# Output-projection weights: three plain quarters split on chip by every tile instead of stored split

## The chip, the cores and the metric

The kernel runs on one core of one Trainium2 chip. The metric is the device time of one execution in microseconds. The kernel before takes 2673.55 us (median of 3 runs, 2673.15 to 2673.85). The five compute engines of the core are named as in the profile: PE multiplies matrices (PEld is its weight loading), DVE is the vector engine, ACT the scalar engine, POOL the general-purpose engine, and SP issues the DMA transfers. Each engine works through its own list of instructions in order, and waits on semaphores for the others.

## The reference, cut to what matters

The reference is a two-layer encoder trunk on a sequence of 2048 rows and width 1024, all in float32. Layer A is a gated mixer. From its result a shared K and V are projected. Layer B is a chunked band attention with a gate, an output projection and a residual, and a last norm follows.

```
q, z = jnp.split(h @ w_qz, 2, axis=-1)
...
p = jax.nn.softmax(sc, axis=-1).astype(vc.dtype)
return jnp.einsum('bhqk,bkhd->bqhd', p, vc)
...
return (o * jax.nn.silu(z)) @ w_out
```

The change concerns only the last matrix product, with the 1024 x 1024 weight `w_out` of layer B, which the kernel knows as `wb_out`.

## The kernel before

**Tiles and pairs.** Layer B works on four tiles t = 0 to 3 of 512 rows. In each tile it goes through eight pairs p = 0 to 7 of attention heads (heads 2p and 2p+1). For a pair, PE projects Q, K and the gate (`pj`), forms the scores (`s`), transposes the normalised probabilities (`tp`) and multiplies them with V (`pv`). For each 128-row block of a head, DVE adds the bias and takes the row extreme (`pr` and `nm`), ACT applies the exponential, DVE inverts the sum (`sl`), POOL scales the row (`pr`), PE transposes, ACT copies the transposed block out (`pt`) and DVE subtracts the copy from it to get its low part (`pt`). The output projection of tile t-1 (`bo`) is dealt out in small portions among the pairs of tile t. `SHARE` says how many portions go into which pair. The last tile's own output projection (`bo_`, function `last_all`) comes at the end.

**Number format.** A float32 operand is split into a high part, which is a cast to fp32r on ACT, and a low part, which is a subtraction on DVE. Each product is then three matmuls: high by high, high by low, low by high.

**Output projection by seven products.** The weight is cut into four quarters b11, b12, b21, b22, each 512 x 512, and each quarter into halves q = 0, 1 of 128 partitions x 1024 elements (512 KB). A tile's product is Strassen's scheme with seven products in the order 1, 7, 2, 6, 5, 4, 3. Products 1, 2 and 3 use a plain quarter of the weight (b11, b21, b22). Products 4 to 7 use sums of quarters.

**Where the split weights come from.** During the first four pairs of tile t = 1, `o_sums` loads the quarters in four units of 128 x 512 each, lets POOL form the sums, splits all seven operands (cast on ACT, subtraction on DVE, tiles `so`), and stores high and low part in DRAM, in `ows[ph, q]`. From then on `o_right(t)` loads four tiles per product, `wh_bo` and `wl_bo` for q = 0 and 1, each 512 KB, straight into the ring with tag "T". That ring has 8 buffers, and the split projection weights `wh_b` and `wl_b` of the attention pairs live in it too. In the last tile `last_right` places weights in various buffers that are free by then. There product 2 alone already loads its plain quarter raw and splits it.

**The projection weights of a pair.** `weights` loads a 512 KB raw tile (`raw_b`) into the ring with tag "wr", which has 2 buffers (`raw_w`), and `split_in` casts it on ACT (`wh_b`, line 230 before) and subtracts on DVE (`wl_b`, line 231 before).

**What sets the order.** The code is written as generators that are interleaved by counts. A scheduler then orders each engine's list. All loads and stores named here are issued by SP, so a load whose buffer is not yet free holds up what stands behind it in SP's list. `on_beat` and `paced_by_pj` tie an instruction to the order of a PE instruction.

Names in the profile have their tile numbers left out: `wl_bo` is the low weight of any tile's output projection, `wlbo` or `wbo` that of the last tile.

Of the kernel before, what the change touches and what calls it, by code (L numbers as in the profile page):

```python
# [9 lines left out]
F32 = mybir.dt.float32  # L10
# [7 lines left out]
P = 128  # L18
# [15 lines left out]
def trunk_kernel(  # L34
# [19 lines left out]
    nc = tc.nc  # L54
# [10 lines left out]
    }  # L65
    ows = {
        (ph, q): dram.tile([P, 2, 1024], F32, name=f"ows{ph}_{q}")
        for ph in range(1, 8) for q in range(2)
    }
    owf = [dram.tile([P, 1024], F32, name=f"owf{q}") for q in range(2)]  # L70
    khd = [
        [dram.tile([2, P, T], F32, name=f"khd{t}_{p}") for p in range(NPAIR)]
        for t in range(NT - 1)
# [121 lines left out]
    def on_beat(ins):  # L195
        if beat:
            tc.add_manual_dep(
                ins.ins, beat[-1],
                mybir.DependencyInfo(mybir.DependencyClass.NoSync, mybir.DependencyReason.DATA),
                reason="order",  # L200
            )
        return ins
# [21 lines left out]
    def raw_w(t, name):  # L224
        if t:
            return raws[0].tile([P, 1024], F32, tag="wr", name=name, bufs=2)
        return sh.tile([P, 1024], F32, tag="raw", name=name, bufs=4)

    def split_in(raw, wh, wl):
        hi = nc.scalar.copy(wh[:], raw[:])  # L230
        tv(wl[:], raw[:], wh[:].bitcast(F32), op=sub)  # L231
        return hi
# [22 lines left out]
        return w  # L255

    o_early = {}

    def o_right(t):
        def right(ph):  # L260
            if (t, ph) in o_early:
                return o_early.pop((t, ph))
            out = []
            for q in range(2):
                name = f"bo{t}_{ph}_{q}"
                w = [w_tile(f"w{i}_{name}") for i in "hl"]
                for i in range(2):
                    nc.sync.dma_start(w[i][:].bitcast(F32), ows[ph, q][:, i, :])
                out.append(w)
            return out  # L270
        return right
# [68 lines left out]
    def o_sums(u, place, s_place):  # L340

        q, i = divmod(u, 2)
        cs = slice(i * 512, i * 512 + 512)
        w = {}
        for rc in ((0, 0), (0, 1), (1, 1), (1, 0)):
            w[rc] = place(f"wo{u}_{rc[0]}{rc[1]}")
            paced_by_pj(nc.sync.dma_start(w[rc][:], wb_out[rc[0], rc[1], q][:, cs]))
        b11, b12, b21, b22 = (w[k][:] for k in ((0, 0), (0, 1), (1, 0), (1, 1)))

        pend = []  # L350

        def stores():
            while pend:
                on_beat(nc.sync.dma_start(*pend.pop(0)))

        def keep(ph, src):
            stores()
            if ph == 5:
                pend.append((owf[q][:, cs], src))
            hi, lo = (s_place(f"so{u}_{ph}{x_}") for x_ in "hl")  # L360
            on_beat(nc.scalar.copy(hi[:], src))
            tv(lo[:], src, hi[:].bitcast(F32), op=sub)
            for n, y_ in enumerate((hi, lo)):
                pend.append((ows[ph, q][:, n, cs], y_[:].bitcast(F32)))

        def first():
            keep(1, b11)
            on_beat(tg(b11, b12, b11, op=sub))
            on_beat(tg(b12, b22, b12, op=sub))

        def second():
            keep(3, b22)
            on_beat(tg(b22, b22, b11, op=sub))

        def third():
            keep(2, b21)
            on_beat(tg(b21, b21, b22, op=sub))

        return [first, second, third] + [
            lambda ph=ph, o=o: keep(ph, o)  # L380
            for ph, o in ((5, b11), (7, b12), (6, b22), (4, b21))
        ] + [stores]

    with ExitStack() as actx:
        ca = actx.enter_context(tc.tile_pool(name="ca", bufs=1))

# [885 lines left out]
    with ExitStack() as bctx:  # L1272
# [310 lines left out]
        def last_right(ph, q):  # L1583
            name = f"bo_{ph}_{q}"
            if ph == 5:
                v = sb.tile([P, 8, 256], F32R, tag="V", name=f"w{name}", bufs=2)
                w = [v[:, i * 4 : i * 4 + 4, :].rearrange("p a b -> p (a b)") for i in range(2)]
            elif ph == 3:
                if q == 0:
                    lw["pt"] = sb.tile([P, 5376], F32R, tag="PT", name=f"w{name}", bufs=1)  # L1590
                w = [lw["pt"][:, (2 * q + i) * 1024 : (2 * q + i + 1) * 1024] for i in range(2)]
            elif ph == 2:
                w = [
                    sh.tile([P, 1024], F32R, tag="raw", name=f"w{i}{name}", bufs=4)[:]
                    for i in "hl"
                ]
            else:
                w = [w_tile(f"w{i}{name}")[:] for i in "hl"]
            if ph == 2:
                raw = raw_w(NT - 1, f"raw_{name}")  # L1600
                nc.sync.dma_start(raw[:], wb_out[1, 0, q])
                nc.scalar.copy(w[0], raw[:])
                tv(w[1], raw[:], w[0].bitcast(F32), op=sub)
            else:
                for i in range(2):
                    nc.sync.dma_start(w[i].bitcast(F32), ows[ph, q][:, i, :])
            lw[ph, q] = w
# [232 lines left out]
        first = ahead(0, 0)  # L1840
# [105 lines left out]
```

## Time and profile before

| what | value |
|---|---|
| median of 3 runs | 2673.55 us |
| the profiled execution, its own time | 2677.64 us |
| its span on the core | 2675.7 us |
| mean granted PE clock | 0.993 |
| PE busy | 2615.7 us, 98% |
| DVE busy | 1872.6 us, 70% |
| ACT busy | 1288.6 us, 48% |
| POOL busy | 895.9 us, 33% |
| DMA queue q1 | 735.19 MB, 79.9% of 16 engines |

The profile is of one execution. Its own time is 4.09 us above the median of the runs, and 1.9 us above its span. Times in its rows are microseconds from the start of the span. Layer B's tile 1 begins at about 1690 us, and everything that the change touches lies between there and the end. A busy PE is not PE at its peak, since matmuls overlap and their ends are modelled, so lost PE time is read from stretches in which PE is not busy and from the granted clock.

### The profile page before, as it was taken

What the parts mean: (1) busy time and instruction counts of PE and PEld (TensorE: products, weight loads), DVE (VectorE), ACT (ScalarE), POOL (GpSimd) and SP (SyncE); (2) the same over time, 40 slices, a digit from 0 to 9 for tenths busy, and PEclk for the clock granted to TensorE, in tenths of its full rate; (3) what the DMA queues carried; (4) which work ended last, traced back from release to release, by engine and by line L of the source; (5) the groups of instructions that cost most, each with busy time, mean ns of one, the idle gap of its engine ahead of it and who ended that gap; (6) DMA issues with size and microseconds to landing.
All of it is one profiled execution on the core that took longest, in us unless ns stands there. A gap on an engine that the chain in (4) does not pass through costs nothing. (4 is left out here: it accounts for less than half of the span.)

```text
span 2675.7 us, 38056 instructions
## 1 busy us (share of the span) xinstructions
PE 2615.7 (98%) x12960; PEld 2187.7 (82%) x12960; DVE 1872.6 (70%) x2934; ACT 1288.6 (48%) x2293; POOL 895.9 (33%) x874
## 2 busy tenths in 40 slices
PE   8999999999999999999999999999999999999997
PEld 7888888888888888888878778887888888888886
DVE  5655676766777577757776767787767677877676
ACT  5422242443433435433355456666655555655563
POOL 3511335152252413104134344333343233323235
PEclk9999999999999999999999999999999999999999
DMA  7899999989988879858676587789788766875678
GB/s 295 314 323 333 348 363 326 320 309 360 325 311 295 311 243 332 319 193 286 255 260 221 188 266 224 233 288 302 252 275 278 247 210 213 265 233 181 205 227 298
DMA packets 281057, 737.61 MB, mean 276 GB/s; under 512 B 29600, under 2 KB 69536, under 8 KB 280864
## 3 DMA queue, kind: packets, MB, share of 16 engines
q1 hardware_dynamic: 280864, 735.19, 79.9%
q8 instruction: 103, 1.69, 0.2%
q14 instruction: 90, 0.74, 0.1%
HBM read 542.65 MB, written 181.93 MB: 271 GB/s over the span
## 5 line engine op out<-in xcount | busy, mean ns | idle before, releaser
L113 PE MATMUL P<-T,S 128*128 128x512 f32 x1248 | 496.2, 398 | 2.0 <-ACT S L434 2.0
L115 PE MATMUL P<-T,S 128*128 128x512 f32 x1248 | 490.4, 393 | 0.0
L114 PE MATMUL P<-T,S 128*128 128x512 f32 x1248 | 489.1, 392 | 1.1 <-DVE T L437 1.1
L1405 POOL TENSOR_SCALAR pr<-pr,sl 128x640 f32<-128x640 f32 (+4 forms) x256 | 202.7, 792 | 528.9 <-DVE sl L1404 468.7
L113 PE MATMUL pj<-hh_b,wh_b 128*128 128x512 f32 x768 | 318.5, 415 | 0.0
L115 PE MATMUL pj<-hh_b,wl_b 128*128 128x512 f32 x768 | 305.5, 398 | 3.6 <-DVE wl_b L231 3.4
L114 PE MATMUL pj<-hl_b,wh_b 128*128 128x512 f32 x768 | 303.4, 395 | 0.0
L1401 ACT ACTIVATE pr<-pr,nm 128x640 f32<-128x640 f32 (+4 forms) x256 | 195.4, 763 | 176.0 <-DVE nm L1394 174.0
L115 PEld LDWEIGHTS P<-T,S 128*128 128x128 f32 x1248 | 235.4, 189 | 50.3
L113 PEld LDWEIGHTS P<-T,S 128*128 128x128 f32 x1248 | 235.8, 189 | 47.0 <-ACT S L434 2.2
L114 PEld LDWEIGHTS P<-T,S 128*128 128x128 f32 x1248 | 235.8, 189 | 46.9 <-DVE T L437 1.3
L1426 DVE TENSOR_TENSOR pt<-tp,pt 128x640 fp32r<-128x640 f32 (+4 forms) x256 | 188.3, 736 | 46.0 <-ACT pt L1425 43.6
L1394 DVE CUSTOM_DVE_ANT_0 pr<-s,bias 128x640 f32<-128x640 f32 (+4 forms) x256 | 187.9, 734 | 41.9 <-PE s L1386 37.4
L1425 ACT CAST pt<-tp 128x640 fp32r<-128x640 f32 (+4 forms) x256 | 158.8, 620 | 53.0 <-PE tp L1421 50.2
L1421 PE MATMUL tp<-ident,pr 128*128 128x128 f32 x1120 | 167.2, 275 | 11.0 <-DVE pt L1426 8.6
L115 PEld LDWEIGHTS pj<-hh_b,wl_b 128*128 128x128 f32 x768 | 144.8, 189 | 37.6 <-DVE wl_b L231 6.0
L1421 PEld LDWEIGHTS tp<-ident,pr 128*128 128x128 f32 x1120 | 131.0, 141 | 45.3 <-issue 18.2
L1446 PEld LDWEIGHTS pv<-pt,V 128*128 128x128 f32 x896 | 145.1, 191 | 25.1 <-DVE pt L1426 6.2
L1446 PE MATMUL pv<-pt,V 128*128 128x256 f32 (+3 forms) x896 | 157.4, 323 | 5.7 <-DVE pt L1426 3.8
L113 PEld LDWEIGHTS pj<-hh_b,wh_b 128*128 128x128 f32 x768 | 145.8, 190 | 18.8 <-ACT wh_b L230 1.4
L114 PEld LDWEIGHTS pj<-hl_b,wh_b 128*128 128x128 f32 x768 | 145.8, 190 | 17.4
L231 DVE TENSOR_TENSOR wl_b<-raw_b,wh_b 128x1024 fp32r<-128x1024 f32 x96 | 125.2, 1305 | 29.1 <-ACT wh_b L230 27.5
(297 smaller groups left out, 5698.6 us busy)
## 6 DMA issues: line engine op xcount, KB each, us to landing
S<-hsd SPq DMA_DIRECT2D x288, 512.0 KB, 5.5
rw<-in_w_a SPq DMA_DIRECT2D x108, 512.0 KB, 6.4
A<-ytd SPq DMA_DIRECT2D x72, 512.0 KB, 5.8
raw_b<-wk SPq DMA_DIRECT2D x72, 512.0 KB, 4.3
hsd<-S SPq DMA_DIRECT2D x56, 512.0 KB, 4.3
V<-vhd SPq DMA_DIRECT2D x56, 512.0 KB, 5.4
wh_bo<-ows SPq DMA_DIRECT2D x42, 512.0 KB, 5.3
wl_bo<-ows SPq DMA_DIRECT2D x42, 512.0 KB, 5.8
```

The costliest lines, as they stand in the source:

```text
L113: first = mm(ps, lh, rh, start=first, stop=False)
L114: mm(ps, lh, rl, start=False, stop=False)
L115: mm(ps, ll, rh, start=False, stop=last)
L231: tv(wl[:], raw[:], wh[:].bitcast(F32), op=sub)
L1394: nc.vector.tensor_tensor_reduce(out=pr[:, c0:].rearrange("p (a b) -> p a b", a=nseg), in0=ps[:, :nseg, :w], in1=bias[:, c0:].rearrange("p ...
L1401: nc.scalar.activation(pr[:, c0:], pr[:, c0:], AF.Exp, scale=-1.0, bias=nm[:], accum_out=sl[:])
L1405: nc.gpsimd.tensor_scalar(pr[:, c0:], pr[:, c0:], sl[:], 1.0, op0=ALU.mult, op1=ALU.mult)
L1421: ins = tpose(tp[:, b, :], pr[:, b * P : (b + 1) * P], ident[:])
L1425: nc.scalar.copy(oh, tp[:, b0:5, :].rearrange("p a b -> p (a b)"))
L1426: nc.vector.tensor_tensor(pt[:, 2560 + o + b0 * P : 2560 + o + 640], tp[:, b0:5, :].rearrange("p a b -> p (a b)"), oh.bitcast(F32), op=ALU ...
L1446: mm(po[:, q0 * P : q1 * P], vtl[t, p][:, i, hs], rhs, start=(i == blocks[0] and j == 0), stop=(i == 7 and j == 1),)
```

## The change

`ows` keeps only products 4 to 7, the four sums. For products 1, 2 and 3 every tile now loads the plain quarter raw from the weight itself, two loads of 512 KB instead of four, into the 2-buffer "wr" ring, and splits it with `split_in` into the same T buffers as before. `o_sums` no longer splits and stores the three plain quarters, so per unit three casts, three subtractions and six stores of 256 KB go. A seventh store, of the raw sum for product 5 into `owf`, which nothing read, goes as well. The POOL sums now run one after the other in the first places of a unit. In the last tile products 1 and 3 are loaded raw and split as product 2 already was.

Counted over the program: in `o_sums` 12 casts and 12 subtractions of 128 x 512 go, with 28 stores of 256 KB. Added are 22 casts and 22 subtractions of 128 x 1024: 18 of each in tiles 0 to 2 and 4 in the last tile. In tiles 0 to 2, 18 raw loads take the place of 36 loads, and in the last tile 4 take the place of 8, all of 512 KB.

```diff
--- before.py
+++ after.py
@@ -65,9 +65,8 @@
     }
     ows = {
         (ph, q): dram.tile([P, 2, 1024], F32, name=f"ows{ph}_{q}")
-        for ph in range(1, 8) for q in range(2)
+        for ph in range(4, 8) for q in range(2)
     }
-    owf = [dram.tile([P, 1024], F32, name=f"owf{q}") for q in range(2)]
     khd = [
         [dram.tile([2, P, T], F32, name=f"khd{t}_{p}") for p in range(NPAIR)]
         for t in range(NT - 1)
@@ -255,6 +254,7 @@
         return w
 
     o_early = {}
+    o_raw = {1: (0, 0), 2: (1, 0), 3: (1, 1)}
 
     def o_right(t):
         def right(ph):
@@ -264,8 +264,13 @@
             for q in range(2):
                 name = f"bo{t}_{ph}_{q}"
                 w = [w_tile(f"w{i}_{name}") for i in "hl"]
-                for i in range(2):
-                    nc.sync.dma_start(w[i][:].bitcast(F32), ows[ph, q][:, i, :])
+                if ph in o_raw:
+                    raw = raw_w(1, f"raw_{name}")
+                    nc.sync.dma_start(raw[:], wb_out[o_raw[ph]][q])
+                    split_in(raw, *w)
+                else:
+                    for i in range(2):
+                        nc.sync.dma_start(w[i][:].bitcast(F32), ows[ph, q][:, i, :])
                 out.append(w)
             return out
         return right
@@ -355,32 +360,21 @@
 
         def keep(ph, src):
             stores()
-            if ph == 5:
-                pend.append((owf[q][:, cs], src))
             hi, lo = (s_place(f"so{u}_{ph}{x_}") for x_ in "hl")
             on_beat(nc.scalar.copy(hi[:], src))
             tv(lo[:], src, hi[:].bitcast(F32), op=sub)
             for n, y_ in enumerate((hi, lo)):
                 pend.append((ows[ph, q][:, n, cs], y_[:].bitcast(F32)))
 
-        def first():
-            keep(1, b11)
-            on_beat(tg(b11, b12, b11, op=sub))
-            on_beat(tg(b12, b22, b12, op=sub))
-
-        def second():
-            keep(3, b22)
-            on_beat(tg(b22, b22, b11, op=sub))
-
-        def third():
-            keep(2, b21)
-            on_beat(tg(b21, b21, b22, op=sub))
-
-        return [first, second, third] + [
-            lambda ph=ph, o=o: keep(ph, o)
-            for ph, o in ((5, b11), (7, b12), (6, b22), (4, b21))
+        def combine(o, x_, y_):
+            return lambda: on_beat(tg(o, x_, y_, op=sub))
+
+        return [
+            combine(b11, b12, b11), combine(b12, b22, b12), combine(b22, b22, b11),
+            lambda: (keep(5, b11), on_beat(tg(b21, b21, b22, op=sub))),
+        ] + [
+            lambda ph=ph, o=o: keep(ph, o) for ph, o in ((7, b12), (6, b22), (4, b21))
         ] + [stores]
-
     with ExitStack() as actx:
         ca = actx.enter_context(tc.tile_pool(name="ca", bufs=1))
 
@@ -1596,9 +1590,9 @@
                 ]
             else:
                 w = [w_tile(f"w{i}{name}")[:] for i in "hl"]
-            if ph == 2:
+            if ph in o_raw:
                 raw = raw_w(NT - 1, f"raw_{name}")
-                nc.sync.dma_start(raw[:], wb_out[1, 0, q])
+                nc.sync.dma_start(raw[:], wb_out[o_raw[ph]][q])
                 nc.scalar.copy(w[0], raw[:])
                 tv(w[1], raw[:], w[0].bitcast(F32), op=sub)
             else:
```

**SP's list at product 3 of tile 0.** Here `bo0_3_0` is tile 0, product 3, half 0; `oc0` and `or0` are pieces of tile 0's result, `x2d0` its place in DRAM, `x1d0` the residual, and `reld` the attention bias. Before:

```order
L268 DMA wl_bo0_4_0_18741<-ows4_0_108 128x1024
L268 DMA wh_bo0_4_1_18744<-ows4_1_109 128x1024
L268 DMA wl_bo0_4_1_18745<-ows4_1_109 128x1024
L1483 DMA x2d0_1_155<-oc0_110_18710 128x512
L1665 DMA oc0_111_18770<-x1d0_60 128x512
L1665 DMA or0_101_18777<-x1d0_60 128x512
L1665 DMA or0_011_18780<-x1d0_60 128x512
L1363 DMA bias1_15_18807<-reld15_181 128x640
L268 DMA wh_bo0_3_0_18851<-ows3_0_106 128x1024
L1483 DMA x2d0_3_157<-oc0_111_18770 128x512
L268 DMA wl_bo0_3_0_18852<-ows3_0_106 128x1024
```

and now, in SP's list, the raw quarter's two loads:

```order
L273 DMA wl_bo0_6_1_18288<-ows6_1_107 128x1024
L244 DMA raw_b1_7_0_18438<-wk7_0_85 128x1024
L1477 DMA x2d0_0_146<-oc0_000_18254 128x512
L1659 DMA oc0_001_18311<-x1d0_60 128x512
L269 DMA raw_bo0_3_0_18777<-in_wb_out 128x1024
L177 DMA xr_b2_0_18914<-xtd2_140 128x4x256
L1477 DMA x2d0_2_148<-oc0_001_18311 128x512
L269 DMA raw_bo0_3_1_18783<-in_wb_out 128x1024
L1337 DMA V1_7_18523<-vhd0_134 128x1024
```

The loads for product 3 stood behind the store of `oc0_111`, which is late in the tile. They now stand ahead of the loads for products 5 and 4, between the stores of product 2's results. What comes later is the split, in ACT's list (its DVE half stands at a like place), where `pt1_13` and `pr1_14` are the softmax of heads 13 and 14:

```order
L1419 CAST pt1_13_18591<-tp1_13_1_18647 128x640
L1674 ACTIVATE jk0_110_18655,ssq0_1_18638<-oc0_110_18634 128x512
L229 CAST wh_bo0_3_0_18775<-raw_bo0_3_0_18777 128x1024
L1395 ACTIVATE pr1_14_0_18681,sl1_14_0_18683<-pr1_14_0_18681,nm1_14_0_18682 128x640
L333 CAST Sho0_4_1_18724<-A0_11_18191 128x512
L1419 CAST pt1_13_18591<-tp1_13_2_18707 128x640
L229 CAST wh_bo0_3_1_18781<-raw_bo0_3_1_18783 128x1024
```

The casts stand in the middle of that softmax, with the exponential and the copy of transposed blocks behind each of them.

**SP's list ahead of the last tile.** `A_hh` are the last tile's left operands, read from DRAM (`ogd3`), `bo2_3` and `bo2_4` weights of tile 2's last products. Before:

```order
L268 DMA wh_bo2_4_1_25032<-ows4_1_109 128x1024
L268 DMA wl_bo2_4_1_25033<-ows4_1_109 128x1024
L268 DMA wh_bo2_3_0_25112<-ows3_0_106 128x1024
L1483 DMA x2d2_3_165<-oc2_111_25054 128x512
L268 DMA wl_bo2_3_0_25113<-ows3_0_106 128x1024
L268 DMA wh_bo2_3_1_25116<-ows3_1_107 128x1024
L1483 DMA x2d2_1_163<-ou2_7_0_23208 128x512
L268 DMA wl_bo2_3_1_25117<-ows3_1_107 128x1024
L1532 DMA A_hh_25120<-ogd3_153 128x1024 x2
L1532 DMA A_hh_25120<-ogd3_153 128x512 x2
L1487 DMA x2d2_3_165<-ou2_7_1_23569 128x512
```

and now:

```order
L273 DMA wh_bo2_4_1_24980<-ows4_1_103 128x1024
L273 DMA wl_bo2_4_1_24981<-ows4_1_103 128x1024
L1526 DMA A_hh_25072<-ogd3_145 128x1024
L1477 DMA x2d2_3_157<-oc2_111_25002 128x512
L1526 DMA A_hh_25072<-ogd3_145 128x1024
L1526 DMA A_hh_25072<-ogd3_145 128x512
L1477 DMA x2d2_1_155<-ou2_7_0_23152 128x512
L1526 DMA A_hh_25072<-ogd3_145 128x512
L1595 DMA raw_bo_1_0_25198<-in_wb_out 128x1024
```

The four loads for `bo2_3` are gone from this place, since their raw loads stand earlier, and the loads of `A_hh` moved up behind `wl_bo2_4_1`.

**DVE's list at the end of the program.** `row0` to `row3` are the four row blocks of the last tile's result, `bo_4` and `bo_3` its last products, `Qlo` the low parts of left operands, and `rr_f` the norm factor. Before:

```order
L1751 TENSOR_TENSOR ou3_1_1_25463<-bo_5_1_25700,ou3_1_1_25463 128x512
L331 TENSOR_TENSOR Qlo_3_0_25732<-A_hl_25121,Qho_3_0_25731 128x512
L331 TENSOR_TENSOR Qlo_3_1_25760<-A_hl_25121,Qho_3_1_25759 128x512
L1768 TENSOR_TENSOR row1_25559<-bo_4_0_25724,ou3_7_0_25520 128x512
L1768 TENSOR_TENSOR row3_25561<-bo_4_1_25752,ou3_7_1_25573 128x512
L1700 TENSOR_TENSOR rr_f3_1_25744<-ssq3_1_25694 128x1
L127 TENSOR_SCALAR rr_f3_1_25744<-rr_f3_1_25744 128x1
L1718 SCALAR_TENSOR_TENSOR row1_25559<-row1_25559,rr_f3_1_25744,gf_13539 128x512 x2
L1700 TENSOR_TENSOR rr_f3_3_25772<-ssq3_3_25718 128x1
L127 TENSOR_SCALAR rr_f3_3_25772<-rr_f3_3_25772 128x1
L1718 SCALAR_TENSOR_TENSOR row3_25561<-row3_25561,rr_f3_3_25772,gf_13539 128x512 x2
L1768 TENSOR_TENSOR row0_25490<-bo_3_0_25780,ou3_1_0_25423 128x512
```

and now:

```order
L1597 TENSOR_TENSOR wbo_3_0_25568<-raw_bo_3_0_25569,wbo_3_0_25568 128x1024
L1762 TENSOR_TENSOR row1_25515<-bo_4_0_25684,ou3_7_0_25476 128x512
L336 TENSOR_TENSOR Qlo_3_0_25692<-A_hl_25073,Qho_3_0_25691 128x512
L1597 TENSOR_TENSOR wbo_3_0_25568<-raw_bo_3_1_25573,wbo_3_0_25568 128x1024
L1694 TENSOR_TENSOR rr_f3_1_25704<-ssq3_1_25654 128x1
L336 TENSOR_TENSOR Qlo_3_1_25720<-A_hl_25073,Qho_3_1_25719 128x512
L126 TENSOR_SCALAR rr_f3_1_25704<-rr_f3_1_25704 128x1
L1762 TENSOR_TENSOR row3_25517<-bo_4_1_25712,ou3_7_1_25529 128x512
L1712 SCALAR_TENSOR_TENSOR row1_25515<-row1_25515,rr_f3_1_25704,gf_13531 128x512 x2
L1694 TENSOR_TENSOR rr_f3_3_25732<-ssq3_3_25678 128x1
L126 TENSOR_SCALAR rr_f3_3_25732<-rr_f3_3_25732 128x1
L1762 TENSOR_TENSOR row0_25446<-bo_3_0_25740,ou3_1_0_25379 128x512
```

The split of `wbo_3` (two subtractions) entered the list, `row1` moved ahead of `Qlo_3_0`, and `row0` no longer waits behind the scaling of `row3`.

## The prediction

> **What bounds the kernel now.** I read the summary first, then the waits of PE from 1690 us on, then busy time in stretches of 25 us, then single instructions around each loss. The summary's first row says that PE is the bound:
>
> ```profile
> PE 2615.7 (98%) x12960; PEld 2187.7 (82%) x12960; DVE 1872.6 (70%) x2934; ACT 1288.6 (48%) x2293; POOL 895.9 (33%) x874
> ```
>
> The matmuls stay as many as they are. So only what PE loses, and what stands behind its last matmul, can change the time. The losses after 1690 us, by releaser (columns: total, times, longest):
>
> ```profile
> PE tp L1421 <- DVE pt L1426: 6.5, 10, 2.2
> PE bo L114 <- DMA wl_bo<-ows: 4.7, 3, 2.3
> PE pv L1446 <- DVE pt L1426: 3.3, 3, 1.4
> PE pj L115 <- DVE wl_b L231: 2.9, 2, 2.3
> PE pv L1446 <- ACT pt L1425: 1.8, 1, 1.8
> ```
>
> The second row is a wait for exactly the weights that the change touches. The others are the softmax and the weight splits, which compete for ACT and DVE. The stretches (busy time of PE, PEld, DVE, ACT, POOL, each with a count, then granted clock, DMA share, GB/s) place them:
>
> ```profile
> 1675.00:1700.00 25.00, 24.67 (x130) 20.63 (x129) 18.09 (x44) 16.12 (x38) 10.57 (x16) 1.00 0.72 229
> ...
> 1775.00:1800.00 25.00, 23.66 (x128) 19.42 (x127) 21.60 (x40) 17.27 (x31) 11.26 (x14) 1.00 0.88 299
> 1800.00:1825.00 25.00, 24.20 (x136) 20.08 (x135) 19.52 (x37) 16.77 (x32) 8.76 (x11) 1.00 0.92 312
> 1825.00:1850.00 25.00, 22.98 (x132) 19.48 (x131) 19.63 (x38) 17.17 (x33) 7.65 (x13) 1.00 0.96 309
> 1850.00:1875.00 25.00, 22.67 (x117) 18.44 (x116) 18.54 (x32) 15.62 (x27) 9.74 (x11) 0.93 0.86 283
> ...
> 1950.00:1975.00 25.00, 22.87 (x122) 19.14 (x121) 14.93 (x28) 14.26 (x28) 10.25 (x11) 1.00 0.82 257
> ...
> 2000.00:2025.00 25.00, 21.69 (x107) 18.00 (x106) 15.66 (x30) 13.65 (x27) 7.52 (x9) 0.93 0.84 279
> 2025.00:2050.00 25.00, 23.78 (x128) 20.08 (x126) 22.69 (x38) 14.99 (x26) 11.43 (x11) 1.00 0.86 297
> ...
> 2600.00:2625.00 25.00, 22.79 (x124) 19.67 (x123) 21.00 (x41) 13.83 (x31) 15.32 (x16) 0.93 0.98 354
> ```
>
> The sums are made between 1700 and 1875 us. There DVE, ACT and DMA are all fuller than before or after, and PE loses 0.8 to 2.3 us per stretch against 0.33 in the quiet row at 1675. Three stretches also ran at a clock of 0.93, each after a stall of some 2 us. I count 7% of 25 us, 1.75 us, for such a clock.
>
> **Term 1, the sums.** A unit loses three casts and three subtractions of these groups (mean ns before the second bar), and seven stores:
>
> ```profile
> L361 ACT CAST so_1h<-wo 128x512 fp32r<-128x512 f32 x4 | 2.5, 622 | 0.1
> ...
> L362 DVE TENSOR_TENSOR so_1l<-wo,so_1h 128x512 fp32r<-128x512 f32 x4 | 2.8, 692 | 0.1
> ...
> L362 DVE TENSOR_TENSOR so_2l<-wo,so_2h 128x512 fp32r<-128x512 f32 x4 | 2.9, 737 | 0.0
> ...
> L362 DVE TENSOR_TENSOR so_3l<-wo,so_3h 128x512 fp32r<-128x512 f32 x4 | 4.4, 1111 | 0.0
> ```
>
> That is 12 x 0.62 = 7.4 us of ACT and 2.8 + 2.9 + 4.4 = 10.1 us of DVE. None of it is on PE's path by itself. What it costs there is what the four stretches from 1775 to 1875 lose above the quiet row: 1.01 + 0.47 + 1.69 + 2.00 = 5.2 us, with the clock 6.9. The dearest of these stalls reads:
>
> ```profile
> 1853.56 1.19 SPq L354 DMA_DIRECT2D ows<-so_1h  x1
> ...
> 1856.77 0.81 SPq L245 DMA_DIRECT2D raw_b<-wk  x1
> ...
> 1863.93 1.04 ACT L230 CAST wh_b<-raw_b 128x1024 fp32r<-128x1024 f32 x1 [3.02 <-DMA raw_b<-wk]
> 1865.00 0.69 ACT L1425 CAST pt<-tp 128x640 fp32r<-128x640 f32 x1
> ...
> 1865.74 0.50 PE L1446 MATMUL pv<-pt,V 128*128 128x512 f32 x1 [1.76 <-ACT pt L1425]
> ```
>
> A raw weight took 7.1 us among the stores of `so_1` and `so_3`. Its cast held up ACT, the copy `pt` stood behind the cast, and `pv` waited for that. The stores go, so I take most of it: -5.0 us, between 0 (POOL's sums and the other four splits stay in the same pairs) and -6.9.
>
> **Term 2, the late plain weights.** The two big waits of PE for `wl_bo` are both for plain quarters, products 2 and 3 of tile 0:
>
> ```profile
> 1956.47 0.50 PE L114 MATMUL bo<-wl_bo,Sho 128*128 128x512 f32 x1 [2.00 <-DMA wl_bo<-ows]
> ...
> 2009.42 0.50 PE L114 MATMUL bo<-wl_bo,Sho 128*128 128x512 f32 x1 [2.25 <-DMA wl_bo<-ows]
> ```
>
> Their stretches lose 25 - 22.87 = 2.13 and 25 - 21.69 = 3.31 us, with the clock in the second 5.44 + 1.75 = 7.2. They are late because the load cannot start before PE gives a T buffer back, and then takes its time:
>
> ```profile
> SPq L268 <- PE pj L115: 70.2, 25, 6.1
> ...
> DMA to landing us min/median/max: 3.7/5.8/8.8
> ...
> L231 DVE TENSOR_TENSOR wl_b<-raw_b,wh_b x75: 1204/1225/2339, 1690.1 to 2573.0; 128x1024 fp32r<-128x1024 f32 x75
> ...
> L230 ACT CAST wh_b<-raw_b x75: 1030/1049/1065, 1689.0 to 2571.9; 128x1024 fp32r<-128x1024 f32 x75
> ```
>
> Before, buffer to weight is 5.8 us. Afterwards the raw tile can be there already, since it needs a "wr" buffer and not a T buffer, and from buffer to weight are a cast of 1.05 and a subtraction of 1.23 us, 2.3 us. That is 3.5 us less, more than either wait. I take -7.0 us, between 0 and -7.2.
>
> **Term 3, the 22 new splits.** They put 22 x 1.05 = 23.1 us on ACT and 22 x 1.33 (99.5 us over 75 in the group of `wl_b` with its slow ones; 29.2) on DVE, in stretches from 1880 to 2660 us. In stretches like 1675, where DVE is busy for 18 of 25 us, PE is nearly full, so part of them is hidden by waiting room in the softmax. For a price per split I take all that PE waited in this part for `pt` and `wl_b`, 6.5 + 3.3 + 2.9 + 1.8 = 14.5 us, over the 75 splits that are there now: 0.19 us. Times 22: +4.3 us, between 0 and 1 us each (+22, the bound that the first rival needs).
>
> **Term 4, the tail.** The stall around 2611 us starts from the transfers of `A_hh`, issued behind the `bo2_3` loads:
>
> ```profile
> 2598.55 0.95 SPq L1532 DMA_DIRECT2D A_hh<-ogd  x1
> ...
> 2607.15 2.54 POOL L1539 TENSOR_TENSOR A_hl<-A_hh 128x512 f32<-128x512 f32 x2 [5.89 <-DMA A_hh<-ogd]
> ...
> 2611.47 1.75 DVE L1718 SCALAR_TENSOR_TENSOR y<-y,rr_f,gf 128x512 f32<-128x512 f32 x1 [0.56 <-POOL rr_f L128]
> ...
> 2613.14 0.81 DVE L1426 TENSOR_TENSOR pt<-tp,pt 128x640 fp32r<-128x640 f32 x1
> ```
>
> POOL's sum `A_hl` came late, behind it the norm factor of `y`, behind that on DVE `y` itself, and behind `y` the `pt` that PE waited for. With `A_hh` issued about 7 us earlier and `pt` ahead of `y`, I count -2.0 of this stretch's 2.21 + 1.75, because four new splits enter a DVE that is busy for 21 of 25 us here. After the last matmul the chain ends on DVE:
>
> ```profile
> 2664.94 1.42 DVE L1718 SCALAR_TENSOR_TENSOR row<-row,rr_f,gf 128x512 f32<-128x512 f32 x2 [0.66 <-POOL rr_f L128]
> ...
> 2666.27 1.28 DVE L1768 TENSOR_TENSOR row<-bo,ou 128x512 f32<-128x512 f32 x2
> ```
>
> `row0` and `row2` stood behind the scaling of `row3`. Now `row0` goes ahead of it, and one scaling (1.42) with part of a hand-over leaves the path: -1.7 us. Together -3.7, between -5.7 (all of both) and +3 (two of the new splits, 2 x 1.3 us, land on the path at `wbo_3`).
>
> **The rest.** 18 loads of 512 KB fewer up to 2600 us (two for one, 9.4 MB) and 4 fewer in the last tile cost nothing and are worth nothing by themselves, since SP and DMA are hidden except where named. The stretch at 2025, where DVE is busy for 22.69 of 25 us, sees its casts in another order, with `A` loads earlier: 0, between -1 and +2.
>
> **The sum.** -5.0 - 7.0 + 4.3 - 3.7 = -11.4 us. The profiled execution took 2677.64 us, 4.09 above the median of the runs, and its span is 2675.7. The terms are differences, so the profiled one would come to 2666.2 and the median to 2673.55 - 11.4 = 2662.2 us.
>
> **A price for meeting POOL.** One row speaks against term 3, a split beside a long operation of POOL:
>
> ```profile
> 2268.16 3.52 POOL L1758 TENSOR_TENSOR ou<-ou,or 128x512 f32<-128x512 f32 x2
> ...
> 2268.19 2.34 DVE L231 TENSOR_TENSOR wl_b<-raw_b,wh_b 128x1024 fp32r<-128x1024 f32 x1
> ```
>
> The subtraction took 2.34 us against the median of 1.225 quoted above. The mean of 1.33 says that this is rare: 0.10 us on average, already in term 3. If each of the 22 met POOL in this way, they would cost 22 x 1.11 = 24.4 us, in place of 4.3 (fourth rival).
>
> The Trainium skill, page "SBUF — State Buffer", section "SBUF: two separate sides", says that a vector operation with two operands in SBUF and a GpSimd operation that reads SBUF hold a shared pair of ports exclusively, the loser waiting for the whole instruction. This row agrees with that, and the new subtractions are of this kind; the median of the other rows says that most do not meet such an operation.
>
> **Rivals.** First, slower: the wait for a free T buffer moves from SP, where nothing but transfers stands behind it, to ACT. If a new cast finds its buffer or its raw tile late, the exponential and `pt` stand behind it, as at 1863.93 us. There it cost 2.0 us of PE and 1.75 of clock, 3.75 us. The gains are 15.7 us, so from five casts in 22 on it decides. Six would cost 22.5: 2673.55 - 15.7 + 22.5 = 2680.4 us. Against it: today ACT's casts wait little:
>
> ```profile
> ACT wh_b L230 <- PE pj L114: 15.7, 11, 1.8
> ```
>
> Second, no change: term 1 is 0 because POOL's sums set the stalls there, term 2 gives 5 and the tail nothing: -5 + 4.3, 2672.9 us. Third, the shared 2-buffer ring makes the pairs' own raw weights late. SP already waits for it:
>
> ```profile
> SPq L245 <- DVE wl_b L231: 34.5, 11, 9.4
> ```
>
> PE's longest wait for `wl_b` is 2.3 us. Six such waits, 13.8, give 2673.55 - 11.4 + 13.8 = 2676.0 us. Fourth, every new subtraction meets POOL and takes 2.34 in place of 1.23 us, and PE pays that: -15.7 + 22 x 1.11 = +8.7, 2682.3 us. Fifth, all terms at their good ends and the splits hidden: -6.9 - 7.2 - 5.7 = -19.8, 2653.8 us.
>
> **Chances.** Forecast 0.48, first 0.14, second 0.17, third 0.10, fourth 0.04, fifth 0.07. About 0.2%, 5.3 us, can be told from no change. Faster takes the forecast but 0.01 and the fifth, 0.54; same takes that 0.01, the second and most of the third, 0.25; slower the rest, 0.21. The range is 2652 to 2680. It takes in the fifth and reaches up to the first, leaving out the fourth, half of the first and what lies beyond. The forecast's own range is 2656 to 2668.
>
> **What would show it.** Term 1: PE over 24 in the stretches from 1775 to 1875. Term 2: no PE wait for products 2 and 3 of tile 0, and `wl_bo` on DVE near 1.3 us. Term 3: PE's waits for `pt` up by some 4 us. Term 4: `A_hl` started some 5 us or more ahead of its place among the rows around it, and the last scaling nearer to the last matmul. The prediction is wrong if ACT stands idle before casts of `wh_bo` for more than 1 us each, with PE waiting for `pt` behind them.

## The result

The changed kernel takes 2661.46 us (median of 6 runs, 2659.12 to 2664.78) against 2673.68 us for the kernel before (6 runs, 2672.29 to 2678.3). The ratio is 0.9949, with a 95% interval of 0.9938 to 0.9960: 12.2 us, or 0.5%, faster. Two later comparisons on other chips gave 0.9938 (0.9925 to 0.9951) and 0.9953 (0.9940 to 0.9967), with medians 16.9 and 13.6 us apart. The profiled execution took 2663.55 us, its span 2661.8 us, 13.9 us below the span before.

### The profile after, by stages

The milestones in both traces are the first transposition of head 0 in tile 1 (the sums begin around it), tile 0's first output product, the first transposition of tile 2, the one of head 13 in tile 3 (the tail begins), and the last matmul. The view of stretches, cut near these points, shows per stretch the busy time of PE, PEld, DVE, ACT and POOL with counts, then clock, DMA share and GB/s. Before:

```profile
1750.00:1910.00 160.00, 153.24 (x836) 128.00 (x835) 126.49 (x230) 104.78 (x189) 56.95 (x71) 0.99 0.90 292
1910.00:2059.00 149.00, 142.33 (x752) 121.04 (x751) 102.87 (x187) 84.11 (x154) 56.36 (x63) 0.99 0.81 267
2059.00:2583.00 524.00, 517.05 (x2835) 443.56 (x2833) 380.20 (x693) 304.79 (x552) 154.91 (x211) 1.00 0.68 219
2583.00:2664.00 81.00, 78.55 (x393) 65.53 (x391) 58.22 (x104) 38.88 (x80) 42.39 (x40) 0.98 0.88 322
```

After:

```profile
1748.00:1898.00 150.00, 149.20 (x838) 127.98 (x837) 119.28 (x221) 99.59 (x179) 58.04 (x70) 1.00 0.82 261
1898.00:2040.00 142.00, 140.54 (x756) 120.05 (x754) 109.13 (x189) 87.94 (x159) 57.42 (x63) 1.00 0.79 260
2040.00:2566.00 526.00, 517.85 (x2828) 443.73 (x2827) 387.88 (x702) 312.43 (x561) 156.42 (x210) 1.00 0.66 208
2566.00:2652.00 86.00, 79.63 (x395) 65.24 (x393) 70.94 (x116) 46.55 (x89) 47.06 (x41) 0.98 0.78 273
```

The same matmuls, to a few records that the cuts move, take 10 us less during the sums and 7 us less in tile 0's product, and 5 us more in the tail. DVE shows where the work went: 7.2 us less during the sums, 6.3 more in tile 0's product, 7.7 more in tiles 2 and 3, and 12.7 more in the tail, where the six new subtractions alone take 10.9 us.

The exact times between the milestones, from every trace of this case (us; the last matmul is taken at its start; the runs are told below):

| kernel | sums | tile 0's product | tiles 2, 3 | tail, PE | after the last matmul |
|---|---|---|---|---|---|
| before | 159.7 | 149.1 | 524.3 | 80.7 | 11.9 |
| changed, three profiles | 149.2, 149.9, 149.9 | 141.9, 141.9, 142.1 | 527.1, 521.9, 522.9 | 85.0, 85.1, 84.9 | 10.5, 10.4, 10.4 |
| e1, sums as before | 159.6 | 141.6 | 522.9 | 85.1 | 10.8 |
| e2, last tile only | 158.0 | 149.4 | 525.0 | 84.9 | 9.5 |
| e3, sums only | 149.7 | 146.6 | 524.4 | 81.7 | 11.8 |
| e4, stores only | 152.8 | 147.7 | 524.8 | 81.9 | 11.8 |
| e5, tail stored | 149.5 | 142.8 | 523.7 | 80.8 | 11.8 |
| e6, only tile 2 stored | 149.7 | 142.1 | 521.4 | 86.7 | 9.5 |
| e7, subtraction twice | 148.9 | 143.8 | 527.8 | 85.3 | 10.5 |
| e9 and its repetition | 149.5, 149.0 | 142.3, 141.4 | 522.3, 522.6 | 81.4, 81.3 | 11.8, 11.8 |
| e10, one tile split | 149.6 | 144.2 | 525.1 | 80.8 | 11.9 |

What stands before the first milestone is the same work in all of them, and still the first milestone lies between 1746.1 and 1751.0 us. That scatter is not the change's. Of the 13.9 us in span, 1.9 are of this kind.

### Where PE was held up before and is not now

The same stretches of 25 us as in the prediction, of the changed kernel:

```profile
1775.00:1800.00 25.00, 25.00 (x145) 21.98 (x144) 18.95 (x38) 16.47 (x31) 12.71 (x16) 1.00 0.82 266
1800.00:1825.00 25.00, 25.00 (x142) 21.34 (x141) 20.71 (x38) 16.54 (x30) 12.65 (x15) 1.00 0.81 259
1825.00:1850.00 25.00, 24.46 (x141) 20.93 (x140) 19.49 (x37) 16.23 (x29) 9.14 (x12) 1.00 0.91 302
1850.00:1875.00 25.00, 25.00 (x144) 21.63 (x143) 21.45 (x41) 19.43 (x37) 9.27 (x12) 1.00 0.74 232
...
1950.00:1975.00 25.00, 25.00 (x139) 21.80 (x138) 16.46 (x31) 13.40 (x25) 7.77 (x9) 1.00 0.94 301
1975.00:2000.00 25.00, 24.00 (x127) 20.11 (x126) 22.42 (x40) 15.23 (x31) 14.96 (x14) 1.00 0.93 330
2000.00:2025.00 25.00, 24.57 (x130) 20.67 (x129) 21.35 (x35) 18.14 (x31) 10.98 (x9) 1.00 0.84 274
...
2575.00:2600.00 25.00, 21.82 (x111) 18.36 (x110) 23.57 (x37) 16.72 (x32) 17.04 (x14) 0.93 0.84 285
```

PE is nearly full during the sums and at 1950 us, where it waited for a plain weight. From 1975 to 2025 us, where the second such wait was, it now loses 1.43 us. The new loss stands at 2575 us, with DVE busy for 23.57 of 25 us. PE's waits from 1690 us on no longer have a row for `wl_bo` loaded from `ows` (the third profile of this kernel has one wait of 1.0 us). Those for `pt` come to 10.3 us, where they were 11.6; the four longest rows are:

```profile
PE tp L1415 <- DVE pt L1420: 6.8, 7, 2.6
PE pv L1440 <- DVE pt L1420: 3.5, 4, 1.5
PE pj L114 <- DVE wl_b L230: 2.3, 2, 1.9
PE bo L112 <- ACT Qho L333: 1.8, 2, 1.3
```

### What came in its place

Two places of the changed kernel are new losses. The first is at the start of tile 3, in this profile (the lines are of several engines, in order of time; `wh_bo` is the cast of product 1's second half in tile 2):

```profile
2342.20 0.38 SPq L269 DMA_DIRECT2D raw_bo<-in_wb_out  x1
...
2348.86 1.05 ACT L229 CAST wh_bo<-raw_bo 128x1024 fp32r<-128x1024 f32 x1 [3.57 <-DMA raw_bo<-in_wb_out]
2349.81 0.57 ACT L1322 CAST K<-pj 64x512 fp32r<-64x512 f32 x1
...
2352.44 0.69 ACT L1419 CAST pt<-tp 128x640 fp32r<-128x640 f32 x1
2353.79 0.81 DVE L1420 TENSOR_TENSOR pt<-tp,pt 128x640 fp32r<-128x640 f32 x1
...
2354.75 1.01 PE L1415 MATMUL tp<-ident,pr 128*128 128x128 f32 x5 [1.95 <-DVE pt L1420]
```

The raw tile took 6.6 us to land, ACT stood idle for 3.57 us at its cast, and K's cast, the scores and `pt` stood behind it. The way from the first transposition of head 1 in tile 3 to that of head 2 grew from 14.53 us to 18.24. This is the prediction's first rival, once. The other two profiles of the changed kernel show it smaller (14.8 and 15.0 us), so it depends on when the transfer lands.

The second is the tail:

```profile
2578.60 3.86 POOL L1752 TENSOR_TENSOR ou<-ou,or 128x512 f32<-128x512 f32 x2
2579.00 2.32 DVE L230 TENSOR_TENSOR wl_bo<-raw_bo,wh_bo 128x1024 fp32r<-128x1024 f32 x1
...
2582.64 1.68 DVE L230 TENSOR_TENSOR wl_bo<-raw_bo,wh_bo 128x1024 fp32r<-128x1024 f32 x1
...
2587.14 2.70 POOL L1533 TENSOR_TENSOR A_hl<-A_hh 128x512 f32<-128x512 f32 x2
...
2587.28 0.67 ACT L1419 CAST pt<-tp 128x640 fp32r<-128x640 f32 x1
...
2587.39 2.74 DVE L1555 SCALAR_TENSOR_TENSOR A_hh<-og,Z 128x256 f32<-128x256 f32 x2
...
2590.16 0.82 DVE L1420 TENSOR_TENSOR pt<-tp,pt 128x640 fp32r<-128x640 f32 x1
...
2591.13 1.30 PE L1415 MATMUL tp<-ident,pr 128*128 128x128 f32 x5 [2.59 <-DVE pt L1420]
```

Two splits beside POOL's long operations took 2.32 and 1.68 us, and a copied block of head 14 waited from 2587.95 to 2590.16 us for DVE. PE stood idle for 2.59 us ahead of the next transposition. DVE was at two operations that write a part of `A_hh`. They took 2.74 us, and the same two took 0.76 us in the kernel before:

```profile
2602.39 0.76 DVE L1561 SCALAR_TENSOR_TENSOR A_hh<-og,Z 128x256 f32<-128x256 f32 x2
```

The loads of `A_hh` were issued early as predicted, and so POOL's sum `A_hl` started 20.8 us after the beginning of the tail, where it was 24.1 us. It thereby came to run beside these two operations. With the loads late, as in e2, e5 and e6 below, the sum starts at 24.2 to 24.7 us and the two operations take 0.8 us.

### The profile page after: what moved, and what is told of

Same layout as the page of the kernel before. It is cut to its first block, busy times and chain, and to the rows that moved or that the text cites. A ratio compares the mean times of both kernels' runs of the same rounds, so it can differ in the third digit from the quotient of the medians.

```text
span 2661.8 us, 37994 instructions
## 1 busy us (share of the span) xinstructions
PE 2610.2 (98%) x12960; PEld 2185.0 (82%) x12960; DVE 1886.4 (71%) x2944; ACT 1302.8 (49%) x2303; POOL 901.7 (34%) x874
## 5 line engine op out<-in xcount | busy, mean ns | idle before, releaser
L1399 POOL TENSOR_SCALAR pr<-pr,sl 128x640 f32<-128x640 f32 (+4 forms) x256 | 210.8, 824 | 531.3 <-DVE sl L1398 460.1
L230 DVE TENSOR_TENSOR wl_b<-raw_b,wh_b 128x1024 fp32r<-128x1024 f32 x96 | 124.0, 1293 | 25.2 <-ACT wh_b L229 24.1
```

Source lines behind the costliest of these rows:

```text
L1399: nc.gpsimd.tensor_scalar(pr[:, c0:], pr[:, c0:], sl[:], 1.0, op0=ALU.mult, op1=ALU.mult)
```

## The experiments

### Which part of the gain is the sums': e1, e3, e4

e1 puts the sums' units back as they were, on the changed kernel:

```
-        for ph in range(4, 8) for q in range(2)
+        for ph in range(1, 8) for q in range(2)
...
-            combine(b11, b12, b11), combine(b12, b22, b12), combine(b22, b22, b11),
-            lambda: (keep(5, b11), on_beat(tg(b21, b21, b22, op=sub))),
+        return [first, second, third] + [
```

> The changed kernel, but the sums' units as before: all seven operands are split and stored, and the stored plain quarters are read by nobody. It takes term 1 away and leaves terms 2 to 4. By the prediction's size of term 1 (5.0 us of the 12 gained) about 2666.5 us. By what the two traces show at the first output-projection product (12.4 us ahead there, 10.5 of them won during the sums) about 2671.5 us. If the raw loads alone were the gain, about 2662 us.

Measured: 2669.65 us against 2675.85 before, ratio 0.9975 (0.9964 to 0.9985). About half of the gain is left, and the sums take 159.6 us again.

e3 keeps the sums' units of the changed kernel and takes the splits away:

```
-                    raw = raw_w(1, f"raw_{name}")
-                    nc.sync.dma_start(raw[:], wb_out[o_raw[ph]][q])
-                    split_in(raw, *w)
+                    for i in range(2):
+                        nc.sync.dma_start(w[i][:].bitcast(F32), ows[stand[ph], q][:, i, :])
...
```

> Term 1 alone: the sums' units of the changed kernel, with no new split anywhere. Products 1, 2 and 3 load four tiles of 512 KB as before, but from the stored sums of products 5, 7 and 6, so the output is not the reference's. By the prediction's size of term 1 about 2668.6 us, by the traces (10.5 us won during the sums) about 2663.2 us, and 2673.7 us if the sums' part is worth nothing.

Measured: 2665.96 us against 2675.85, ratio 0.9963 (0.9950 to 0.9976), 9.9 us. The sums take 149.7 us, as in the changed kernel.

e4 is e3 with the casts and subtractions back and the stores left out. Its units keep the order that they had before, POOL's sums between the splits:

```
-            for n, y_ in enumerate((hi, lo)):
+            for n, y_ in enumerate((hi, lo) if ph > 3 else ()):
...
```

> As the run with the sums alone, but the twelve casts and twelve subtractions stay, and only the 28 stores go (six per unit of the plain quarters, and the raw sum of product 5). Output not the reference's, for the same reason. If the stores held up the raw weights (the 7.1 us load behind the stores of so_1 and so_3), the gain is that of the run with the sums alone, about 2663 us. If ACT and DVE were the limit there, it is small, about 2672 us. If half and half, about 2668 us.

Measured: 2670.97 us against 2675.85, ratio 0.9981 (0.9973 to 0.9990). The sums take 152.8 us. Against the mean of 159.1 us in the three kernels with all seven operands (159.7, 159.6, 158.0), the stores are worth 6.3 us, and the casts and subtractions, with the new order of POOL's sums, 3 us more. The medians put it at half and half: 4.9 us of the 9.9 that e3 has. A row each, of the stretch that was the worst before, first e1, then e4, then e3:

```profile
1825.00:1850.00 25.00, 22.73 (x128) 18.79 (x127) 19.11 (x36) 17.69 (x32) 6.60 (x11) 1.00 0.95 304
```

```profile
1825.00:1850.00 25.00, 24.79 (x141) 20.98 (x141) 19.95 (x39) 17.32 (x33) 7.92 (x12) 1.00 0.83 268
```

```profile
1825.00:1850.00 25.00, 24.47 (x142) 20.94 (x141) 20.22 (x37) 15.56 (x28) 9.64 (x12) 1.00 0.87 289
```

Without the stores the DMA share falls from 0.95 to 0.83 and PE is nearly full, although ACT and DVE have as much to do. The stores stand in SP's list among the loads of the pairs' raw weights, and the traces show that those loads were issued late. In the kernel before, three of them in a row (at 1800, 1813 and 1830 us) were issued 19.1 to 23.3 us after the subtraction that gave their buffer back. In e1 and e2 it is 19.6 to 23.9 us, in e4 0 to 1.5 us, and in e3 and the changed kernel 0 to 4.5 us. The way from issue to landing has less of a part in it: the median of the 14 loads of this stage is 5.6 us before and 5.7 us in e4. ACT's casts waited for the late tiles:

```profile
ACT wh_b L230 <- DMA raw_b<-wk: 6.9, 4, 3.0
```

This is the kernel before from 1750 to 1910 us. It is 5.7 us in e1 and 4.7 us in e2, and e4, e3 and the changed kernel have no such wait in this stage.

### The tail: e2, e5, e6

e2 is the kernel before with the last tile's products 1 and 3 split on chip:

```
-            if ph == 2:
+            if ph in o_raw:
                 raw = raw_w(NT - 1, f"raw_{name}")
-                nc.sync.dma_start(raw[:], wb_out[1, 0, q])
+                nc.sync.dma_start(raw[:], wb_out[o_raw[ph]][q])
```

> The kernel before, with only the last tile's products 1 and 3 loaded raw and split. By the prediction (term 4 at -3.7 and four of the splits at 0.19 us each) about 2670.5 us. By the theory that the tail of the changed kernel loses PE time to the new splits and wins some of it back behind the last matmul, 2673 to 2677 us.

Measured: 2675.09 us against 2675.85, ratio 1.0002 (0.9992 to 1.0011): no difference. In the trace PE's tail is 4.2 us longer than before (84.9 against 80.7) and the end 2.4 us shorter (9.5 against 11.9). PE waits 1.46 us for the split `wbo` of product 3 some 5 us before the last matmul, which is the bad end that term 4 named.

e5 lets tile 1 store the parts of products 1 and 3 that it has split, and the tail load them:

```
                     split_in(raw, *w)
+                    if t == 1 and ph != 2:
+                        for i in range(2):
+                            kept.append((ows[ph, q][:, i, :], w[i][:].bitcast(F32)))
...
-                if ph in o_raw:
+                if ph in o_raw and (t, ph) != (2, 3):
...
-            if ph in o_raw:
+            if ph == 2:
```

> The changed kernel, but tile 1, after splitting products 1 and 3 of its own, stores the split parts (eight stores of 512 KB, one pair of tile 2 later), and product 3 of tile 2 and products 1 and 3 of the last tile load them from there. Six of the 22 splits go, all in the tail. By the theory that the splits in the tail cost more than their reordering wins (95.5 us from the transposition of head 13 to the end in the changed kernel, 92.6 before), 2 to 4 us faster than the changed kernel, 15 us below the kernel before. By the prediction's term 4 (the tail is a gain of 3.7 us less 6 x 0.19) 2.6 us slower than the changed kernel, 9.5 us below before. If the stores disturb tile 2, the first less 1 to 2 us.

Measured: 2659.92 us against 2676.46, ratio 0.9934 (0.9922 to 0.9946). The changed kernel on the same chip had 2659.53 (e8). In the trace the tail is as before, 80.8 + 11.8 us, so 2.9 us shorter than the changed kernel's 85.1 + 10.4. The medians don't show it.

e6 takes this only for product 3 of tile 2, so that the last tile's splits stay:

```
+                    if t == 1 and ph == 3:
...
-                if ph in o_raw:
+                if ph in o_raw and (t, ph) != (2, 3):
```

> As the run before, but only product 3 of tile 2 takes its split parts from tile 1's store; the last tile's products 1 and 3 are loaded raw and split. If the two splits of that product, which meet POOL at 2579 to 2584 us, are the tail's loss (7.2 us of PE there, against 2.8 with the last tile's splits alone), 3 to 4.5 us faster than the changed kernel. If the last tile's splits are the loss, as fast as the changed kernel within 1 us. If the order at the end is worth it only together, 1 us faster.

Measured: 2658.05 us, ratio 0.9927 (0.9914 to 0.9940), 1.5 us below e8. The tail is 86.7 + 9.5 = 96.2 us, no shorter than the changed kernel's 95.5. So the two splits that meet POOL are not what the tail costs by themselves; once they are gone, PE loses as much to the last tile's splits. e2, with these alone, has 94.4 us. Only without both sets (e5) does the tail take 92.6 us.

The clock has a part in these lengths. The mean granted clock of PE's tail is 0.98 before, in e5 and in two profiles of the changed kernel, 0.96 in e6, and 1.00 in e2 and in the third profile of the changed kernel; 0.02 is 1.7 us here. PE's idle time in the tail is free of that: 2.5 us before, 2.6 in e5, 5.9 in e6, 7.0 in e2, and 6.1, 5.9 and 7.2 in the changed kernel. In every kernel that splits products 1 and 3 of the last tile on chip, two waits of PE for `Qho` are in it, 1.8 us together. The longer one in the changed kernel is:

```profile
2627.27 0.50 PE L112 MATMUL bo<-whbo,Qho 128*128 128x512 f32 x1 [1.29 <-ACT Qho L333]
```

The other kernels have neither. From the last head's product with V to this cast of `Qho` pass 4.2 us here and 4.3 us before, so the cast is not slower. Before, PE works on portions of `bo` without a gap in that time; now its list holds too few of them there. This part of the loss is the order of PE's list, which came with the splits.

### What a subtraction costs: e7 and e8

e7 does each new subtraction of tiles 0 to 2 twice, but for product 3 of tile 2:

```
                     split_in(raw, *w)
+                    if (t, ph) != (2, 3):
+                        tv(w[1][:], raw[:], w[0][:].bitcast(F32), op=sub)
```

> The changed kernel with each new subtraction of tiles 0 to 2 done twice (16 more of 128 x 1024; not product 3 of tile 2). It measures what a subtraction on DVE costs there. At the prediction's 0.19 us per split, of which DVE is about half, 1.5 to 3 us slower than the changed kernel. If each put its 1.23 us on PE's path, 20 us. If DVE has room everywhere there, nothing.

e8 is the changed kernel beside it:

> The changed kernel once more, as the base for the three runs beside it, and a second profile of it. If the stall of PE at 2352 us (a cast for product 1 of tile 2 that waits 3.57 us for its raw tile) belongs to the order of the lists, it is here again, and some 3.7 us from the first portion of tile 3 to the next. If it is a matter of when transfers land, it is gone or smaller, as in the run with the sums as before, where the same lists had none. The ratio is 0.9949 within its interval.

Measured: e7 2666.42 us, ratio 0.9960 (0.9945 to 0.9976); e8 2659.53 us, ratio 0.9938 (0.9925 to 0.9951). The medians differ by 6.9 us, which is 0.43 us for each of the 16; the two intervals touch. By the stages of the traces tile 0's product takes 1.9 us more and tiles 2 and 3 take 0.7 to 5.9 more, above all at the start of tile 3 (21.1 us from head 1 to head 2, where e8 has 14.8).

### Fewer splits: e9 to e12

e9 splits in tiles 0 and 1 only. Tile 1 stores its twelve parts, and everything after loads them:

```
-                if ph in o_raw:
+                if ph in o_raw and t <= 1:
...
+                    if t == 1:
+                        for i in range(2):
+                            kept.append((ows[ph, q][:, i, :], w[i][:].bitcast(F32)))
...
-            if ph in o_raw:
+            if ph == 2:
```

> Only tiles 0 and 1 split the plain quarters; tile 1 stores what it split (twelve stores of 512 KB), and tile 2 and the last tile load from there (product 2 of the last tile stays raw, as before). By the theory of the stages: sums 149.5 and tile 0's product 142 us as in the changed kernel, no late raw tile at the start of tile 3 (14.5 us), the tail as before (92.6 us to the end against 95.5): 3 to 4 us faster than the changed kernel, ratio to the kernel before about 0.993. If tile 2's loads into T buffers are late as tile 0's were, each of them 2 us, no gain over the changed kernel.

e10 is the same with tile 0 in the place of tile 1:

> As the run before, but tile 0 alone splits and stores (in the second half of tile 1), and tile 1's product loads from there too. Against the run before it: six splits fewer in tile 2's stretch, and the waits for stored weights there return (0.34 and 0.82 us in the kernel before), and twelve stores of 512 KB in a fuller stretch (DMA share 0.8 to 0.96). By the stages, tile 2's stretch 310.5 instead of 308 us: 1 to 3 us slower than the run before. If the splits in tile 2 cost 0.4 us each, as the run with doubled subtractions says, 1 to 2 us faster instead.

Measured: e9 2654.81 us, ratio 0.9912 (0.9897 to 0.9928); e10 2661.21 us, ratio 0.9940 (0.9925 to 0.9955). In e10 the stage of tile 0's product takes 144.2 us and tiles 2 and 3 take 525.1, 2 and 3 us more than in e9. The waits for stored weights are little of that: 1.1 us in all from 1690 us on, against 0.8 in e9. PE's waits for the pairs' own `wl_b` are 2.6 us against 0.3. e9 and the changed kernel once more, on one chip:

> The run with two tiles split once more, beside the changed kernel on the same chip, to tell the two apart. By the stages (tail 93.2 us against 95.5, start of tile 3 without a late raw tile, 0.3 to 3.8 us) 2.5 to 6 us faster than the changed kernel. If the lower median of its first runs was scatter, within 2 us of it.

> The changed kernel as the base for the run beside it: ratio to the kernel before 0.9938 to 0.9949, and a third profile of the stretch at the start of tile 3 (230.4 and 233.9 us so far for tile 3 up to head 13).

Measured: e9's kernel 2657.85 us, ratio 0.9946 (0.9934 to 0.9959); the changed kernel 2659.26 us, ratio 0.9953 (0.9940 to 0.9967). The traces agree both times that the tail is 2.2 and 2.3 us shorter (81.4 + 11.8 and 81.3 + 11.8, against 85.0 + 10.4). The medians are 1.4 us apart here. e9's kernel is faster than the kernel before in both comparisons. That it is faster than the changed kernel, by some 2 us, the traces say and the times don't settle.

## Why the prediction was right, and where it was not

The forecast was 2662.2 us, and 2661.46 was measured. The sum came out because terms that were wrong in opposite directions largely cancelled, and the nearness of 0.7 us is luck: the two later comparisons put the gain at 16.9 and 13.6 us, and the measured stages of the table add up to -14.5 where 11.4 us were forecast. The table sets the terms, their splits at 0.19 us each included, against the stages (changed kernel, mean of three profiles; before, mean of the profiles in which that stage is unchanged, for the last two rows the kernel before alone).

| step | forecast | measured |
|---|---|---|
| term 1 with 2 splits, the sums | -5.0 + 0.4 | 159.1 to 149.7: -9.4 |
| term 2 with 4 splits, tile 0's product | -7.0 + 0.8 | 149.3 to 142.0: -7.3 |
| 10 splits in tiles 2 and 3 | +1.9 | 524.6 to 524.0: -0.6 |
| tail of PE with 6 splits | -2.0 + 1.1 | 80.7 to 85.0: +4.3 |
| after the last matmul | -1.7 | 11.9 to 10.4: -1.5 |

**Term 1** had the right mechanism and the wrong size, and it lies beyond its bound of -6.9. The mechanism is shown: with the stores of the plain quarters in the list the raw weights came late, and without them (e4) half to two thirds of the gain are there. One point of it was read too narrowly: the row of 7.1 us put the delay into the transfer, and the larger part is the issue, up to 23 us after the buffer came free.

The size was read from PE's busy time by stretches. Between the two traces the stage differs by 10.5 us. PE's idle time is 6.0 of them, from 6.8 us to 0.8. The other 4.5 us stand in its busy time, 153.0 us before and 148.4 after for the same 831 matmuls, and the view of stretches can't show them as a loss. The slow clock that the prediction added is in one of the three profiles with all seven operands; the other two ran this stage at 1.00 and took 159.6 and 158.0 us. The prediction also took 0.33 us off each stretch for a quiet row, and PE is now fuller than that row in three of the four. The section on the profile named the limit of the view, and still the sum of the stretches was taken for the bound. The way between two named matmuls does not depend on how their durations are recorded. (The casts of the sums run from 1751.1 to 1877.1 us, not from 1700; none of the sums hangs on that.)

**Term 2** held: -7.3 us in the stage. PE's wait rows for products 2 and 3 of tile 0 are gone. The run with the stored weights still loaded whole (e3) shows 146.6 us, so some 2.7 us of this stage can come with the sums out of the way. With the sums as before (e1) the splits alone bring 7.5 us, so the two do not add. The reason given was that the raw tile is there before the T buffer is free, and that the split then takes 2.3 us. The raw tiles of products 2 and 3 had landed 10.8 to 28.0 us ahead of their casts, and from the cast's start to the low weight's end passed 2.3 us twice for product 2, and 3.4 and 5.7 us for product 3. The new subtractions of tiles 0 to 2 took 1.37 us on the mean:

```profile
L230 DVE TENSOR_TENSOR wl_bo<-raw_bo,wh_bo 128x1024 fp32r<-128x1024 f32 x18 | 24.6, 1369 | 5.4 <-ACT wh_bo L229 5.3
L229 ACT CAST wh_bo<-raw_bo 128x1024 fp32r<-128x1024 f32 x18 | 18.9, 1049 | 14.1 <-PE pj L113 6.6 <-DMA raw_bo<-in_wb_out 5.7 <-ACT pr L1395 1.0
```

**Term 3** came out below its price in tiles 2 and 3 (between +2.4 and -2.8 us in the three profiles, +1.9 forecast), and e7 gives 0.43 us for a further subtraction, above the 0.19 taken for a whole split. Both fit a DVE with room for the first splits and less for a second set; that is argued, and the interval of e7 is wide. PE's waits for `pt` did not rise by the 4 us that were to show this term. The first rival occurred in part: in each of the three profiles ACT stood idle for 1.3 to 3.6 us before five of the 18 casts of `wh_bo`, as many as the prediction had reckoned it needs. But PE paid 3.7 us for one of them, at 2348.86 us, in one profile, and 0.3 to 0.4 us there in the other two, so it did not decide. The third rival did not occur: PE's waits for `wl_b` are 2.3, 0.2 and 0.5 us, where they were 2.9.

**Term 4** failed in its first half, as the prediction put it: "I count -2.0 of this stretch's 2.21 + 1.75, because four new splits enter a DVE that is busy for 21 of 25 us here." With six splits at 0.19 us, PE's tail was to win 0.9 us, and it lost 4.3. The row of DVE was right, and the stall behind `y` is gone. Two things were wrong. The price for the splits was taken as elsewhere, although DVE is busy for 23.57 of 25 us afterwards, with POOL at 17.04. And the early `A_hl`, counted as a pure gain, ran into DVE's work on `A_hh`, so that a stall of 2.59 us took the place of one of 2.21. The shares of the 4.3 us are the waits told above; e2 and e5 show the splits as their source: the last tile's splits alone cost PE 4.2 us, and without the six splits the 4.3 us are gone, since both the splits and the order that they brought are gone.

The fourth rival, subtractions that meet POOL, took place: five of the 22 new subtractions took 1.7 to 2.3 us, in each of the three profiles, two of them those at 2579.00 and 2582.64 us. e6 shows that these two are not the whole cause. The Trainium skill, page "SBUF — State Buffer", section "SBUF: two separate sides", gives the exclusion of the two engines as complete for the length of an instruction. The trace agrees: POOL's 3.86 us are two operations, the first from 2578.60 to 2580.23 us, and the subtraction that began at 2579.00 ended 1.09 us behind it, where it takes 1.22 us by itself; POOL's second ended 1.15 us behind the subtraction, where the shortest of its kind takes 1.28 us.

The second half of term 4 held: 1.5 us less behind the last matmul, of 1.7 forecast. The last rows of the changed kernel:

```profile
2651.34 0.39 PE L114 MATMUL bo<-wbo,Qlo 128*128 128x512 f32 x1
```

```profile
2654.92 0.68 DVE L1762 TENSOR_TENSOR row<-bo,ou 128x512 f32<-128x512 f32 x1
...
2657.46 1.42 DVE L1712 SCALAR_TENSOR_TENSOR row<-row,rr_f,gf 128x512 f32<-128x512 f32 x2 [0.66 <-POOL rr_f L127]
```

The last scaling starts 6.1 us after the last matmul, where it was 7.4 us.

**Open** stays why e2 and e6 end faster still (9.5 us after the last matmul) with a longer tail before it; their DVE lists are in another order there, and PE's wait of 1.46 us for `wbo` some 5 us earlier gives DVE time to catch up. That this is the reason was not tested. How the 10 splits in tiles 2 and 3 came to cost nothing is open too, since that stage differs by 5 us from profile to profile.

## What to carry to other kernels

A store that nobody waits for can still be dear: it stands in a list of transfers ahead of loads that the engine that sets the time does wait for, and here 28 stores of 256 KB cost 5 to 6 us. Reading less from memory and splitting on chip paid where the engine that splits had room, and not in the last stretch, where six splits, with the order of the lists that came with them, cost PE 4.3 us and won back 1.5 us behind the last matmul. A transfer that comes earlier moves the work behind it as well, here onto a neighbour that it slows. Measure a loss as the time between two named instructions of that engine, not as the gaps in its busy time.

## What was not expected of the hardware

The first milestone, behind 1750 us of work that is the same in all these kernels, lies anywhere between 1746.1 and 1751.0 us, while the stage of the sums agrees within 1.0 us (148.9 to 149.9) over the ten profiles with four operands. Single executions of the changed kernel differ by up to 5.7 us (2659.12 to 2664.78), and those of the kernel before by 13.3 us on one chip (2668.92 to 2682.25, 25 runs). So gains of 2 us were visible in the stages of the traces and not in the times.
